# Where a tuned kernel mixes its gathered expert slots into the dense loop: a new rate, no slot step inside the last key step, and an earlier load of the first norm's weight

## The chip, the cores and the metric

The kernel runs on one core of a Trainium2 chip. The metric is the device time of one launch in microseconds. In the text PE is TensorE's matmul row, PEld its weight loads, DVE is VectorE, ACT is ScalarE, POOL is GpSimd and SP is the engine whose queue issues most loads and stores.

## The reference, cut to what matters

One layer of a decoder runs over 512 prompt tokens, 16 meta tokens and 32 sample tokens. Its last part, PEER, is what most of the change touches: each token picks 16 experts of 16384 in each of 8 heads, and adds their outputs.

```python
h = rmsnorm(x, norm1_w)                      # first norm
...
x = x + mixed @ w_out
# peer(): for each token 8 heads x 16 experts
act = gelu(einsum('thkd,td->thk', u_tab[expert], xb))
return einsum('thk,thkd->td', gate * act, v_tab[expert])
...
y = rmsnorm(x, final_norm_w)
```

## The kernel before, in words

The expert part treats tokens in two ways. Three tiles of 128 prompt tokens are **dense**: all 16384 experts are multiplied for them on PE, in 128 rows of 128 experts. A **key step** for row e (`h_step`) multiplies the row's key weights with the activations, 24 matmuls of 384 columns. A **value step** for row v (`v_step`) adds gate times gelu times value weights to the accumulators `eacc` in PSUM, 36 matmuls of 512 columns that the trace shows as 18 pairs. The two alternate from row 36 on, value row v behind key row v+1; `v_last` does the last value row, finishes the three dense tiles (`finish`: add, sum of squares on ACT, power on POOL, scale, store) and then drains what is left. All weights are fp32, split into a rounded part (`thi`, an ACT cast, L1474) and a residual (`tlo`, a DVE subtraction, L1482).

Two tiles (the 32 samples and the first prompt tile) are **gathered**: `gathered` fetches, for slot k, one expert row per token with an indirect DMA from POOL (L1338, four buffers). It then takes two steps per slot: a dot product on DVE (L1352) with gelu and gate on ACT (L1353, L1354), and one accumulation on DVE (L1359). There are 32 + 128 slots, so 320 steps, and some 15 for finishing the two tiles.

The slot steps come from the task list `fill`. Each `fill.tick(rate)` adds `rate` to a sum and emits one step for each whole unit reached. A key step has four ticks and a value step three. Every engine executes its own instructions strictly in the order in which the program emits them, so the ticks fix the place of each slot step among the dense loop's instructions on DVE and ACT.

I write one loop step of DVE as letters in program order: R is a residual (L1482), D the dot product (L1352), X the accumulation (L1359), M the gate's multiply (L1520), S the residual of the gated activation (L485). Each step begins with the R of a key row, then come the slot steps of the key step's ticks, M, R (of a value row), S, and the slot steps of the value step's ticks. Without slot steps it reads R M R S.

At the start, SP loads the sample tile, prompt tiles and the norm's weight `wbc` (L532, broadcast to 128 partitions) in the order of the calls. `norms` then runs over the tiles in a software pipeline: the sum of squares of tile i (L490 on ACT, L496 on DVE, L498 on POOL) is emitted ahead of the scaling of tile i-1 (L514 on DVE).

Of the kernel before, what the change touches and what calls it, by code (L numbers as in the profile page):

```python
# [90 lines left out]
def body(tc, a):  # L91
# [7 lines left out]
    def pool(st, name, bufs=1, right=False, space=None):  # L99
        kw = {} if space is None else {"space": space}  # L100
        return st.enter_context(tc.tile_pool(name=name, bufs=bufs, side="right" if right else "left", reuse_waits="tile", **kw))

    def load(dst, src):
        nc.sync.dma_start(dst, src)
# [399 lines left out]
    def norms(xs, xp, pm, wbc, out, hi, lo, cols, after):  # L504

        rs, hn, n = {}, {}, len(xs)
        for i in range(n + 2):
            if i < n:
                xt, k, rows = xs[i]
                rs[i] = rstd_of(xp, xt[k], rows)  # L510
            if 0 <= i - 1 < n:
                xt, k, rows = xs[i - 1]
                hn[i - 1] = out(i - 1)
                V.scalar_tensor_tensor(hn[i - 1][:rows], xt[k][:rows], rs[i - 1], wbc[:rows], ALU.mult, ALU.mult)  # L514
            if i - 2 >= 0:
                transpose_split(pm, hn[i - 2], xs[i - 2][2], hi, lo, cols[i - 2])
                after(i - 2)
# [14 lines left out]
    def load_bc(xp, name):  # L532
        t = xp.tile([P, D], F32, name="wbc", tag="wbc", bufs=1)
        load(t, a[name].to_broadcast([P, D]))
        return t
# [271 lines left out]
    def network(ph, keep_h2, wq, es, sq):  # L807
# [159 lines left out]
        with ExitStack() as xs_:  # L967
            xp = pool(xs_, "xp", 1, True)

            def fetch_x(i):  # L970
                xt = xp.tile([P, D], F32, name="xt", tag="xt", bufs=4)
                load(xt[: src[i][0]], src[i][2])
                return xt

            def after_x(i):
                if i + 4 < len(src):
                    xl.append(fetch_x(i + 4))
                if i == 0:
                    s.split(0)
                elif i == 1:  # L980
                    s.split(1)
                elif i == 2:
                    s.begin(0)
                elif i == 3:
                    s.begin(1)

            xl = [fetch_x(i) for i in range(2)]
            wbc = load_bc(xp, "n1w")
            xl += [fetch_x(i) for i in range(2, 4)]
            s.fetch(0)  # L990
            s.fetch(1)
            norms([(xl, i, r) for i, (r, _, _) in enumerate(src)], xp, pm, wbc, lambda i: xl[i], hh, hl, [c for _, c, _ in src],
                  after_x)
# [313 lines left out]
    def finish_load(o, rows, x2):  # L1307
        load(o[:rows], x2)
        return o
# [67 lines left out]
    NE = 128  # L1377
# [14 lines left out]
    Q_RATE, W_RATE = 1, 3  # L1392

    G_AHEAD = 0.38
    G_END = -8
    G_RATE = (2 * 160 + 15 - 3 * (AH - 1) * G_AHEAD) / (7 * (NE - AH) - 3 * G_END)

    def build_w(bp, pw, io, sls, Wt, w0):
# [41 lines left out]
    def experts(h2s, x2s, h2pair, ph, g_tiles, d_tiles, outs, s, ghp, es, sq):  # L1440
# [14 lines left out]
        def ps_h():  # L1455
            return php.tile([P, 512], F32, name="hps", tag="h")
# [3 lines left out]
        def fetch(kind, e):  # L1460
            if e < NE and (kind, e) not in raws:
                t = (dp if kind == "u" else dv).tile([P, D], F32, name="traw", tag="traw" + kind, bufs=2 if kind == "u" else VB)
                load(t, a["uT"][e] if kind == "u" else a["uv"][e * P : (e + 1) * P, D : 2 * D])
                raws[kind, e] = t

        def prep(kind, e, late=False):
            if e >= NE or (kind, e) in sp_:
                return
            fetch(kind, e)
            t = raws[kind, e]  # L1470
            pl, nb = (dp, 2) if kind == "u" else (wtp, VS)
            x = pl.tile([P, D], F32R, name="thi", tag="thi" + kind, bufs=nb)
            y = pl.tile([P, D], F32R, name="tlo", tag="tlo" + kind, bufs=nb)
            AC.copy(x, t)  # L1474
            sp_[kind, e] = x, y
            if not late:
                prep_lo(kind, e)

        def prep_lo(kind, e):
            if e < NE and (kind, e) in raws:  # L1480
                x, y = sp_[kind, e]
                (PO if kind == "u" and e < sum(AQ) else V).tensor_tensor(y, raws.pop((kind, e)), x, ALU.subtract)  # L1482
                if kind == "v" or e + 2 not in (AH, AH + 1) or e >= AH:
                    fetch(kind, e + (2 if kind == "u" else VB))
# [3 lines left out]
        def h_step(e, rate, lo_at=0):  # L1488
            prep("u", e)
            if e + 1 != AH:  # L1490
                fetch("u", e + 1)
                prep("u", e + 1, True)
            x, y = sp_.pop(("u", e))
            ps = ps_h()
            for k in range(KT):
                ks = slice(k * P, k * P + P)
                cs = slice(c0, c0 + nt)
                mm(ps[:, :nt], x[:, ks], hi[:, k, cs], start=(k == 0), stop=False)  # L1498
                mm(ps[:, :nt], x[:, ks], lo[:, k, cs], start=False, stop=False)  # L1499
                mm(ps[:, :nt], y[:, ks], hi[:, k, cs], start=False, stop=(k == KT - 1))  # L1500
                if k % 2:
                    (bg if e < AH else fill).tick(rate)
                if k == lo_at and e + 1 != AH:
                    prep_lo("u", e + 1)
            if e < AT:
                gh[e] = ga.tile([P, nt], F32, name="gh", tag="gh", bufs=AT)
            elif e < AH - 3:
                gh[e] = gbf[:, (e - AT) * nt : (e - AT + 1) * nt]
            else:
                gh[e] = ghp.tile([P, nt], F32, name="gh", tag="gh", bufs=3)  # L1510
            AC.activation(gh[e], ps[:, :nt], AF.Gelu)  # L1511
# [131 lines left out]
        def v_of(v, rate):  # L1643
            if v % 8 == 0:
                fetch_w(v // 8 + 1)
            v_step(v, rate)
# [15 lines left out]
        for v in range(AH - 1, NE - NL):  # L1662
            if v == AH + 1:
                load(T_["fwbc"], a["fw"].to_broadcast([P, D]))
            if v >= AH + 2 and v % 4 == 0 and late:
                i, t = late.popleft()
                fins[t] = finish_load(gb[:, i + 1], rows_of[t], x2s[t])
            if AH < v + 1 < NE:
                h_step(v + 1, G_RATE)
            v_of(v, G_RATE)  # L1670
        for v in range(NE - NL + 1, NE):
            h_step(v, G_RATE)
# [9 lines left out]
    es, sq = ExitStack(), ExitStack()  # L1682
    wq = Stream(None, None, [(WQ0 + i, None, 0, None, PO) for i in range(16)], 4, Q_RATE, 0)
    h2s, x2s, h2pair, ghp = network(ph, g_tiles, wq, es, sq)
    experts(h2s, x2s, h2pair, ph, g_tiles, d_tiles, outs, wq, ghp, es, sq)
    ctx.close()

# [91 lines left out]
```

## Time and profile before

| | us |
|---|---|
| median of 3 runs | 2202.42 (2197.52 to 2209.17) |
| the profiled execution's own time | 2195.1 |
| its span, first to last instruction | 2193.2 |
| PE busy | 2083.8 (95%) |
| PEld busy | 1916.0 (87%) |
| DVE busy | 1570.8 (72%) |
| ACT busy | 864.5 (39%) |

The dense loop with slots runs from about 1362 to 2170 us of the span, the rest of the tail to 2193.2. A busy share is an average over the whole span; which engine sets the pace of a stretch has to be read from waits.

### The profile page before, as it was taken

How to read it: one execution, taken by the hardware profiler on the slowest of the kernel's cores; microseconds unless marked ns; L12 is line 12 of the kernel's file. 1: busy time of each engine (PE TensorE's matmuls, PEld its weight loads, DVE VectorE, ACT ScalarE, POOL GpSimd, SP SyncE). 2: the span in 40 equal slices, each digit the busy share in tenths (PEclk: the TensorE clock that was granted, in tenths of full speed). 3: DMA queues.
4: the chain of work that ended last, by engine and by line, in shares of the span. 5: the costliest groups of instructions: out<-in, count | busy, mean ns of one | idle time of the engine just before them, and what ended most of it. 6: DMA issues, size and time to landing. Idle time of an engine off the chain costs nothing. (4 is left out here: it accounts for less than half of the span.)

```text
span 2193.2 us, 34559 instructions
## 1 busy us (share of the span) xinstructions
PE 2083.8 (95%) x13085; PEld 1916.0 (87%) x13085; DVE 1570.8 (72%) x3084; ACT 864.5 (39%) x1591; POOL 754.6 (34%) x875
## 2 busy tenths in 40 slices
PE   6999999999999998999899999999999999999995
PEld 6988898898999998999899878989888888888884
DVE  6866667546426314899999688778878778887877
ACT  3323343333124323333477434343433443344343
POOL 3497610025442334664166111212222222222221
PEclk9999999999999998999999999999999999999998
DMA  4433334326644233222256999879998899989884
GB/s 151 127 123 112 115 120 154 114 91 205 210 153 123 87 138 123 92 102 73 106 231 269 330 332 331 324 281 357 347 326 304 335 338 338 330 316 336 331 298 162
DMA packets 199813, 478.90 MB, mean 218 GB/s; under 512 B 53440, under 2 KB 114752, under 8 KB 176096
## 3 DMA queue, kind: packets, MB, share of 16 engines
q1 hardware_dynamic: 169136, 278.50, 37.8%
q0 software_dynamic: 24752, 170.67, 20.8%
q10 hardware_dynamic: 5760, 27.53, 3.2%
q8 instruction: 103, 1.69, 0.3%
q14 instruction: 62, 0.51, 0.1%
HBM read 419.42 MB, written 54.46 MB: 216 GB/s over the span
## 5 line engine op out<-in xcount | busy, mean ns | idle before, releaser
L471 PE MATMUL gps<-pr,wh 128*128 128x272 f32 (+1 forms) x3328 | 582.3, 297 | 6.4 <-DVE pr L485 3.8
L471 PEld LDWEIGHTS gps<-pr,wh 128*128 128x128 f32 x3328 | 479.7, 191 | 15.2 <-DVE pr L485 4.7
L1482 DVE TENSOR_TENSOR tlo<-traw,thi 128x1024 fp32r<-128x1024 f32 x241 | 299.2, 1242 | 118.1 <-ACT thi L1474 117.9
L1338 POOL DMA_INDIRECT uv<-in_uv,ei x128 | 186.2, 1455 | 534.7 <-DVE acc L1359 527.2
L1500 PE MATMUL hps<-pr,tlo 128*128 128x384 f32 x1024 | 347.7, 340 | 14.5 <-DVE tlo L1482 13.6
L471 PE MATMUL gps<-pr,wl 128*128 128x272 f32 (+1 forms) x1664 | 353.0, 293 | 2.9 <-DVE wl L437 2.2
L1498 PE MATMUL hps<-pr,thi 128*128 128x384 f32 x1024 | 350.5, 342 | 1.6 <-ACT thi L1474 1.3
L1499 PE MATMUL hps<-pr,thi 128*128 128x384 f32 x1024 | 344.1, 336 | 0.0
L1474 ACT CAST thi<-traw 128x1024 fp32r<-128x1024 f32 x256 | 266.0, 1040 | 25.5 <-PE eacc L1558 17.9
L471 PEld LDWEIGHTS gps<-pr,wl 128*128 128x128 f32 x1664 | 266.3, 192 | 3.8 <-DVE wl L437 2.9
L1558 PE MATMUL eacc<-thi,ghi 128*128 128x512 f32 x768 | 241.7, 396 | 6.8 <-ACT ghi L484 5.8
L1558 PE MATMUL eacc<-tlo,ghi 128*128 128x512 f32 x768 | 241.4, 395 | 3.4
L1558 PE MATMUL eacc<-thi,glo 128*128 128x512 f32 x768 | 237.7, 390 | 0.0
L437 POOL TENSOR_TENSOR wl<-wraw,wh 128x1024 fp32r<-128x1024 f32 x60 | 144.1, 2401 | 247.0 <-ACT wh L436 240.0
L1359 DVE SCALAR_TENSOR_TENSOR acc<-uv,w,acc 128x1024 f32<-128x1024 f32 x158 | 202.4, 1281 | 33.8 <-ACT w L1354 33.8
L1353 ACT ACTIVATE w<-w 128x1 f32<-128x1 f32 x160 | 32.5, 203 | 478.5 <-DVE uv L1352 478.5
L1500 PEld LDWEIGHTS hps<-pr,tlo 128*128 128x128 f32 x1024 | 192.6, 188 | 20.8 <-DVE tlo L1482 19.6
L1498 PEld LDWEIGHTS hps<-pr,thi 128*128 128x128 f32 x1024 | 192.7, 188 | 10.2 <-ACT thi L1474 4.5
L1499 PEld LDWEIGHTS hps<-pr,thi 128*128 128x128 f32 x1024 | 192.8, 188 | 3.5
L1352 DVE SCALAR_TENSOR_TENSOR uv<-uv,h 128x1024 f32<-128x1024 f32 x160 | 195.1, 1220 | 0.7 <-DMA uv<-in_uv,ei_None 0.7
L1558 PEld LDWEIGHTS eacc<-tlo,ghi 128*128 128x128 f32 x768 | 141.5, 188 | 46.3 <-DVE tlo L1482 17.8
L1558 PEld LDWEIGHTS eacc<-thi,ghi 128*128 128x128 f32 x768 | 140.9, 188 | 40.5 <-ACT ghi L484 16.5
(410 smaller groups left out, 3000.3 us busy)
## 6 DMA issues: line engine op xcount, KB each, us to landing
traw<-in_uT SPq DMA_DIRECT2D x128, 512.0 KB, 4.2
traw<-in_uv SPq DMA_DIRECT2D x128, 512.0 KB, 6.7
wraw<-in_W SPq DMA_DIRECT2D x104, 512.0 KB, 3.4
Wt<-wb ACTq DMA_DIRECT2D x24, 1024.0 KB, 4.4
wt<-Wt SPq DMA_DIRECT2D x15, 1536.0 KB, 14.4
st<-in_state_hgrn SPq DMA_DIRECT2D x8, 512.0 KB, 4.4
Wd<-W SPq DMA_DIRECT2D x8, 512.0 KB, 5.0
ATd<-AT SPq DMA_DIRECT2D x8, 512.0 KB, 4.2
```

The costliest lines, as they stand in the source:

```text
L437: E.tensor_tensor(wl, r3, wh, ALU.subtract)
L471: mm(ps[:, b, :w], x[:, k], y[:, k, b * w : b * w + w], start=(k == 0 and x is wh and y is hi), stop=(k == KT - 1 and x is wl))
L1338: PO.indirect_dma_start(out=uvs[j], out_offset=None, in_=a["uv"], in_offset=bass.IndirectOffsetOnAxis(ap=ei[:, k : k + 1], axis=0))
L1352: V.scalar_tensor_tensor(out=uv[:, 0:D], in0=uv[:, 0:D], scalar=1.0, in1=h2, op0=ALU.mult, op1=ALU.mult, accum_out=w)
L1353: AC.activation(w, w, AF.Gelu)
L1359: V.scalar_tensor_tensor(acc, uv[:, D:], w, acc, ALU.mult, ALU.add)
L1474: AC.copy(x, t)
L1482: (PO if kind == "u" and e < sum(AQ) else V).tensor_tensor(y, raws.pop((kind, e)), x, ALU.subtract)
L1498: mm(ps[:, :nt], x[:, ks], hi[:, k, cs], start=(k == 0), stop=False)
L1499: mm(ps[:, :nt], x[:, ks], lo[:, k, cs], start=False, stop=False)
L1500: mm(ps[:, :nt], y[:, ks], hi[:, k, cs], start=False, stop=(k == KT - 1))
L1558: mm(accs[d][:, b], l[:, ds_], r[:, b * 512 : b * 512 + 512], start=st, stop=en)
```

## The change

Three edits. The first prompt tile's load is issued behind the norm's weight rather than ahead of it. `G_END` goes from -8 to 2, which raises `G_RATE` from 295.1/668 = 0.442 to 295.1/638 = 0.463 steps per tick. And the last key step (row 127) gets rate 0 instead of `G_RATE`.

```diff
-            xl = [fetch_x(i) for i in range(2)]
+            xl = [fetch_x(0)]
             wbc = load_bc(xp, "n1w")
-            xl += [fetch_x(i) for i in range(2, 4)]
+            xl += [fetch_x(i) for i in range(1, 4)]
...
-    G_END = -8
+    G_END = 2
     G_RATE = (2 * 160 + 15 - 3 * (AH - 1) * G_AHEAD) / (7 * (NE - AH) - 3 * G_END)
...
             if AH < v + 1 < NE:
-                h_step(v + 1, G_RATE)
+                h_step(v + 1, G_RATE if v + 1 < NE - 1 else 0)
             v_of(v, G_RATE)
```

The number of instructions on DVE, PE and POOL stays the same; their order changes. The first place is DVE at the end of the loop, from the residual of key row 127 before (`traw`, `thi`, `tlo` are a weight row and its parts, `acc` is the gathered tile's sum, `gb` the tile's input and output). Before:

```order
L1482 TENSOR_TENSOR tlo<-traw,thi 128x1024
L1359 SCALAR_TENSOR_TENSOR acc<-uv,w,acc 128x1024
L1520 TENSOR_TENSOR gh<-gh,wt 128x384
L1482 TENSOR_TENSOR tlo<-traw,thi 128x1024
L485 TENSOR_TENSOR glo<-gh,ghi 128x384
L1352 SCALAR_TENSOR_TENSOR uv,w<-uv,h_9361 128x1024
L1359 SCALAR_TENSOR_TENSOR acc<-uv,w,acc 128x1024
L1352 SCALAR_TENSOR_TENSOR uv,w<-uv,h_9361 128x1024
L1359 SCALAR_TENSOR_TENSOR acc<-uv,w,acc 128x1024
L1520 TENSOR_TENSOR gh<-gh,wt 128x384
L1482 TENSOR_TENSOR tlo<-traw,thi 128x1024
L485 TENSOR_TENSOR glo<-gh,ghi 128x384
```

And now, from the last part of key row 126's step, in which the gathered tile is finished already (L1318, L496, L1324), through the rows of key row 127:

```order
L1520 TENSOR_TENSOR gh<-gh,wt 128x384
L1482 TENSOR_TENSOR tlo<-traw,thi 128x1024
L485 TENSOR_TENSOR glo<-gh,ghi 128x384
L1318 TENSOR_TENSOR gb<-gb,acc 128x1024
L496 TENSOR_SCALAR ss<-ss 128x1
L1482 TENSOR_TENSOR tlo<-traw,thi 128x1024
L1324 SCALAR_TENSOR_TENSOR gb<-gb,ss 128x1024
L1520 TENSOR_TENSOR gh<-gh,wt 128x384
L1482 TENSOR_TENSOR tlo<-traw,thi 128x1024
L485 TENSOR_TENSOR glo<-gh,ghi 128x384
L1520 TENSOR_TENSOR gh<-gh,wt 128x384
L1482 TENSOR_TENSOR tlo<-traw,thi 128x1024
```

Before, 11 slot instructions on DVE (five L1352, six L1359) stand behind the residual of key row 127, six of them behind the last S, among the finishing of the dense tiles; now none does.

The second place is DVE inside the loop, at key row 75, from one key row's residual to the next one's. Before (R D X M R S D, then R):

```order
L1482 TENSOR_TENSOR tlo<-traw,thi 128x1024
L1352 SCALAR_TENSOR_TENSOR uv,w<-uv,h_9361 128x1024
L1359 SCALAR_TENSOR_TENSOR acc<-uv,w,acc 128x1024
L1520 TENSOR_TENSOR gh<-gh,wt 128x384
L1482 TENSOR_TENSOR tlo<-traw,thi 128x1024
L485 TENSOR_TENSOR glo<-gh,ghi 128x384
L1352 SCALAR_TENSOR_TENSOR uv,w<-uv,h_9361 128x1024
L1482 TENSOR_TENSOR tlo<-traw,thi 128x1024
```

And now (R X D M R S X D, then R):

```order
L1482 TENSOR_TENSOR tlo<-traw,thi 128x1024
L1359 SCALAR_TENSOR_TENSOR acc<-uv,w,acc 128x1024
L1352 SCALAR_TENSOR_TENSOR uv,w<-uv,h_9361 128x1024
L1520 TENSOR_TENSOR gh<-gh,wt 128x384
L1482 TENSOR_TENSOR tlo<-traw,thi 128x1024
L485 TENSOR_TENSOR glo<-gh,ghi 128x384
L1359 SCALAR_TENSOR_TENSOR acc<-uv,w,acc 128x1024
L1352 SCALAR_TENSOR_TENSOR uv,w<-uv,h_9361 128x1024
L1482 TENSOR_TENSOR tlo<-traw,thi 128x1024
```

Here one slot instruction more has come between the two residuals. Over the 77 steps from the residual of key row 49 to that of key row 126, DVE's order holds six forms, this often:

| form | slot instructions | before | now |
|---|---|---|---|
| R X D M R S X | 3 | 26 | 26 |
| R D X M R S D | 3 | 25 | 22 |
| R D M R S X D | 3 | 10 | 7 |
| R X M R S D X | 3 | 9 | 3 |
| R D X M R S D X | 4 | 5 | 11 |
| R X D M R S X D | 4 | 2 | 8 |
| sum | | 238 | 250 |

The third place is SP's queue at the start, as the difference between the two:

```order
 L104 DMA xt<-in_x_sample 32x1024
-L104 DMA xt<-in_x_prompt 128x1024
 L104 DMA wbc<-in_n1w 128x1024
-L104 DMA xt<-in_x_prompt 128x1024 x2
+L104 DMA xt<-in_x_prompt 128x1024 x3
```

The weight `wbc` is now the second of the tiles' loads and the first prompt tile the third; the loads behind them keep their places.

## Rows read from the trace of the kernel before

**Rows 1.** The page: span, and busy time of each engine.
```profile
span 2193.2 us, 34559 instructions
...
PE 2083.8 (95%) x13085; PEld 1916.0 (87%) x13085; DVE 1570.8 (72%) x3084; ACT 864.5 (39%) x1591; POOL 754.6 (34%) x875
```
**Rows 2.** Busy us by stretch (PE, PEld, DVE, ACT, POOL), granted clock, DMA share, GB/s.
```profile
1480.00:2144.00 664.00, 650.00 (x3201) 569.19 (x3200) 532.34 (x656) 265.20 (x538) 169.50 (x117) 1.00 0.90 330
...
2170.00:2193.20 23.20, 0.00 (x0) 0.00 (x0) 14.52 (x21) 5.88 (x14) 3.13 (x4) 0.59 0.23 90
```
**Rows 3.** Waits of DVE, ACT, PE, 1600 to 2100 us (us, times, longest).
```profile
DVE tlo L1482 <- ACT thi L1474: 52.1, 55, 1.5
DVE gh L1520 <- ACT gh L1511: 26.3, 27, 1.0
DVE acc L1359 <- ACT w L1354: 20.3, 34, 0.6
...
ACT w L1353 <- DVE uv L1352: 273.3, 88, 3.9
...
PE hps L1500 <- DVE tlo L1482: 4.1, 7, 0.7
```
**Rows 4.** DVE in order of time, 2108 to 2154 us.
```profile
2108.25 1.22 DVE L1482 TENSOR_TENSOR tlo<-traw,thi 128x1024 fp32r<-128x1024 f32 x1 [1.53 <-ACT thi L1474]
...
2116.53 1.22 DVE L1482 TENSOR_TENSOR tlo<-traw,thi 128x1024 fp32r<-128x1024 f32 x1
...
2125.54 1.23 DVE L1482 TENSOR_TENSOR tlo<-traw,thi 128x1024 fp32r<-128x1024 f32 x1 [1.54 <-ACT thi L1474]
...
2136.59 1.23 DVE L1482 TENSOR_TENSOR tlo<-traw,thi 128x1024 fp32r<-128x1024 f32 x1 [1.53 <-ACT thi L1474]
...
2144.02 1.22 DVE L1482 TENSOR_TENSOR tlo<-traw,thi 128x1024 fp32r<-128x1024 f32 x1
...
2153.87 1.23 DVE L1482 TENSOR_TENSOR tlo<-traw,thi 128x1024 fp32r<-128x1024 f32 x1 [1.53 <-ACT thi L1474]
```
**Rows 5.** DVE in order of time: a step R D X M R S D X.
```profile
1941.55 1.22 DVE L1482 TENSOR_TENSOR tlo<-traw,thi 128x1024 fp32r<-128x1024 f32 x1
...
1950.81 1.22 DVE L1482 TENSOR_TENSOR tlo<-traw,thi 128x1024 fp32r<-128x1024 f32 x1
```
**Rows 6.** DVE in order of time: key rows 48 and 49.
```profile
1464.32 0.56 DVE L1520 TENSOR_TENSOR gh<-gh,wt 128x384 f32<-128x384 f32 x1 [2.16 <-ACT gh L1511]
...
1469.89 1.22 DVE L1482 TENSOR_TENSOR tlo<-traw,thi 128x1024 fp32r<-128x1024 f32 x1
```
**Rows 7.** The end, in order of time: PE, DVE and ACT.
```profile
2145.90 0.34 PE L1498 MATMUL hps<-pr,thi 128*128 128x384 f32 x1
...
2154.18 0.34 PE L1498 MATMUL hps<-pr,thi 128*128 128x384 f32 x1
...
2165.48 0.73 PE L1558 MATMUL eacc<-thi,ghi 128*128 128x512 f32 x2 [2.14 <-ACT ghi L484]
...
2169.61 0.39 PE L1558 MATMUL eacc<-thi,glo 128*128 128x512 f32 x1
...
2169.43 1.22 DVE L1318 TENSOR_TENSOR gb<-gb,eacc 128x1024 f32<-128x1024 f32 x1
...
2171.64 0.19 ACT L490 ACTIVATION_READ_ACCUMULATOR junk<-gb 128x1 f32 x1
...
2184.08 0.15 DVE L496 TENSOR_SCALAR ss<-ss 128x1 f32<-128x1 f32 x1
...
2184.89 1.28 DVE L1324 SCALAR_TENSOR_TENSOR gb<-gb,ss 128x1024 f32<-128x1024 f32 x1 [0.66 <-POOL ss L498]
```
**Rows 8.** The start, in order of time: ACT and DVE.
```profile
5.38 1.06 ACT L490 ACTIVATE junk<-xt 128x1024 bf16<-128x1024 f32 x1 [0.53 <-DMA xt<-in_x_prompt]
...
7.74 1.27 DVE L514 SCALAR_TENSOR_TENSOR xt<-xt,ss,wbc 32x1024 f32<-32x1024 f32 x1 [1.03 <-DMA wbc<-in_n1w]
...
10.37 0.15 DVE L496 TENSOR_SCALAR ss<-ss 128x1 f32<-128x1 f32 x1 [1.35 <-ACT junk L490]
```
## The prediction
> **What bounds the kernel now.** The page comes first: PE is busy 95% of the span and DVE 72% [rows 1], which reads like a kernel bound by matmuls. The change touches the dense loop with slots, so I read that stretch by itself: over 664 us PE is busy 650.00, its weight loads 569.19, DVE 532.34 [rows 2]. That still names PE.
>
> The waits say otherwise [rows 3]. In 500 us of the loop DVE waits only for ACT: 52.1 us for the cast `thi`, 26.3 for the gelu, 20.3 for the slot's weight, 98.7 together. And ACT's longest wait, 273.3 us, is for DVE's dot product (I found none of either engine for PE or for a transfer there). PE is the one that waits for DVE, 4.1 us for `tlo` alone. So two in-order engines hand work back and forth without regard to PE, and PE follows. The mechanism is in the code: ACT's two small instructions behind each D wait for it, and the casts and the gelu that DVE needs next stand behind those two. A D with R behind it costs a wait of 1.53 or 1.54 us [rows 4], with M behind it at most 1.0, with X behind it at most 0.6 [rows 3].
>
> The timeline confirms it. DVE takes a fixed time from one key row's residual to the next one's, whatever PE does, and it depends only on the form of the step [rows 4, 5]:
>
> - R X D M R S X: 2116.53 - 2108.25 = 8.28 us
> - R D X M R S D: 2125.54 - 2116.53 = 9.01, so 9.00 with the others
> - R X D M R S X D: 2136.59 - 2125.54 = 11.05
> - R X M R S D X: 2144.02 - 2136.59 = 7.43, taken as 7.44
> - R D M R S X D: 2153.87 - 2144.02 = 9.85
> - R D X M R S D X: 1950.81 - 1941.55 = 9.26, taken as 9.27
>
> Other steps of one form agree within 0.02 us. A check: the 77 steps from the residual at 1469.89 [rows 6] to that at 2144.02 [rows 4] last 674.13 us. The counts before give 26 x 8.28 + 25 x 9.00 + 10 x 9.85 + 9 x 7.44 + 5 x 9.27 + 2 x 11.05 = 674.19. PE alone needs 8.28 for such a step (2154.18 - 2145.90) [rows 7], so 637.6 for 77: the DVE stream is 36 us longer than PE's own work.
>
> **The change, part by part.** *The rate.* With the counts of now the same 77 steps last 26 x 8.28 + 22 x 9.00 + 7 x 9.85 + 3 x 7.44 + 11 x 9.27 + 8 x 11.05 = 694.92 us, **20.7 more**. That is for 12 slot instructions more, 1.73 us each: some 1.2 of DVE's time (an R of the same 128x1024 takes 1.22 [rows 4]) and the rest waits for ACT, since the form that multiplies most, with D as its last, is the dearest. No work of PE covers it, because PE is the one that follows.
>
> *Where the loop starts from.* The first gathered tile ends just ahead of key row 48, and there DVE has few slot steps and does wait for PE, by way of the gelu; the last such M is at 1464.32 [rows 6]. Now the tile's end comes about one step earlier, the first prompt slot with it, and that M waits for PE's row alone. From DVE's idle 2.16 us before it I take it as 0.3 us earlier; bounds 0 and 0.6. So the residual of key row 49 moves from 1469.89 to 1469.3 or so (the form around it is also 0.3 shorter), and that of key row 126 from 2144.02 to 2164.2, **+20.2 us**.
>
> *The end.* Before, 2193.2 - 2144.02 = 49.2 us follow that residual. Now PE waits for it as it does before for the residual of key row 127 at 2153.87. From there to PE's end (2169.61 + 0.39 = 2170.0) are 16.1 us, of which 2.14 are PE's wait for `ghi` of the last value row [rows 7]: its gelu stood on ACT behind two slots' weights. No slot stands there now, so the wait goes. With one step of 8.28 more, PE ends 16.1 - 2.1 + 8.3 = 22.3 us behind the residual of key row 126, less about 0.3 for matmuls that slowed at the restart: 22.0. The finished gathered tile's L1318 and L1324 on DVE, 2.5 us, lie beside 8 us of PE work here.
>
> Behind PE's end the dense tiles are finished in turn. The first can start when its accumulator is done, some 2.7 us ahead of PE's end: two of three equal parts of the last value row, which took 4.5 us with its restart (2165.48 to 2170.0). Each has a chain from its add to its scaling: the square's sum is read out 2171.64 + 0.19 - 2169.43 = 2.40 us behind the add's start, and from L496 to the scaling it takes 2184.89 - 2184.08 = 0.81, with the step between 3.3 [rows 7]. Scaling takes 1.2, and the next add stands behind it: scalings start at +0.6, +5.1 and +9.7 us of PE's end, the last of two halves ends at +11.1. Before, the last scaling ended at 2184.89 + 1.28 = 2186.17, 16.2 behind PE's end, and 7.0 us of store and end followed. I keep those 7.0. So 22.0 + 11.1 + 7.0 = 40.1 us follow the residual instead of 49.2: **-9.1 us**. Bounds: -7 if the chains meet something, -11 if the smaller last store ends sooner.
>
> *The start.* DVE waits 1.03 us for `wbc` at 7.74 [rows 8]. But the first scaling also stands behind L496 of the first prompt tile, whose load landed at 5.38 and now comes where `wbc` was. Its square (1.06) then ends near 8.9, and the first scaling starts about 1.3 us later than before instead of earlier. Little of it passes on: the second scaling stands behind L496 at 10.37, which waits for the second prompt tile, and that load keeps its place. I take +0.3 us; bounds -0.5 (the load of `wbc` was what counted) and +1.3 (all of it passes on).
>
> **Sum.** +20.2 - 9.1 + 0.3 = **+11.4 us**: span 2204.6, and the profiled execution's own 2195.1 would be 2206.5. The median shown is 2202.42, 7.3 above that execution; the difference is laid on the median: **2213.8 us**, slower by 0.52%. That is about what a measurement of this kernel can tell from no change (0.5%, 11 us).
>
> **A rule against this reading.** PE is busy 650.00 and its weight loads 569.19 of 664 us [rows 2], more than DVE. The Trainium skill (Perfetto Trace Analysis, Identifying the Most-Contended Engine) takes the engine with the highest occupancy as the one to optimize, TensorE's judged by its weight loads. By that rule PE would bind and the added DVE work would be free, which is the first rival. The waits of this trace [rows 3] disagree.
>
> **The rivals.**
> *PE hides the slots.* If DVE has slack in the loop, the 12 instructions cost nothing there and only the end counts: PE's 2.14 us wait goes and the finishing shrinks from 16.2 to 11.1, so -7.2 in all: 2195.2 us, on the other side. It decides if the mean step now stays at the 8.71 us of before (674.13 / 77). For it speak PE's 95%; against it that PE already waits for DVE. 7%.
> *Only busy time counts.* The 12 instructions cost their 1.2 us each, 14.4, and the waits for ACT stay as many as before in sum: 20.2 becomes 13.9, and the time 2207.5. For it: waits depend on neighbours, and some new pairs of forms (R D X M R S D X followed by R D X M R S D) don't occur before. Against: each form's time was the same behind every other. 14%.
> *The gathered rows come late.* A slot's buffer is fetched when the slot three ahead of it is done, and DMA is busy 0.90 of the loop [rows 2]. Three slots in a dense group now lie closer, and a D that waits 1 us for its row in each of the 12 more crowded steps adds 12 us: 2226. Against: no D waits for a transfer in the loop now, and a step is longer on the whole. 7%.
> *It doesn't do what it says.* Slots could remain behind the last key step; the order on DVE shows none. 2%: the time of before.
>
> **How the numbers follow.** My forecast has 70%, with 2209 to 2218 as its own range: bounds of the end -2 to +2, start -0.8 to +1, loop start 0.3, and 2 to 3 us for the median (the three runs shown lie 12 us apart). The range for 8 in 10 takes in the second rival and part of the third: 2205 to 2221. Slower by over 0.5% (above 2213.4): half of the forecast's 70%, a little more since 2213.8 lies above the line, and the third rival, 46%. Within 0.5%: the other half and most of the other rivals, 50%. Faster by over 0.5% (below 2191.4): 4%, from the first rival with a better end.
>
> **What would show it.** In the changed kernel's trace DVE should need 9.02 us a step (694.9 / 77), each form the time listed, and the residual of key row 126 stand near 2164. PE's busy share of the loop falls to some 95%, with all its waits for DVE and ACT. The 2.14 us wait ahead of the last value row is gone, PE ends near 2186.5, and DVE's last scaling 11 us later. The first scaling starts near 9 us. Wrong would be: steps of 8.71 (PE or slack hides), forms whose time depends on their neighbour, a D that waits for `in_uv`, or a PE start that moves by more than 1 us.

## The result, and the profile after

The changed kernel's median is 2213.0 us (2206.39 to 2221.98, 16 runs) against 2202.24 (2197.52 to 2209.17, 16 runs) of before: ratio 1.0052 [1.004, 1.0064], so 10.8 us slower. The forecast was 2213.8.

The profiled execution took 2221.98 us, 9 above its median. Its span is 26.8 us longer than the one before [rows 1], but 14.0 of these were there ahead of the loop: the residual of key row 36 stands at 1376.12, before at 1362.10. Executions differ by that much there. In the experiments e1, e2 and e8, which have the old code up to there, it stands at 1365.6 to 1368.3, and in e3, which has the new start, at 1372.79; with what each profiled execution lies off its kernel's median taken off, these four, before and after all come to 1367.0 to 1369.8. So I measure every step from a residual inside the loop. The page:

```profile
span 2220.0 us, 34561 instructions
...
PE 2100.1 (95%) x13085; PEld 1921.0 (87%) x13085; DVE 1575.1 (71%) x3084; ACT 864.4 (39%) x1591; POOL 755.6 (34%) x875
```

Busy time by stretch (PE, PEld, DVE, ACT, POOL, then granted clock, DMA share, GB/s), the loop's stretch moved by what its start moved:

```profile
1496.00:2180.00 684.00, 658.20 (x3205) 566.89 (x3203) 545.39 (x674) 268.00 (x552) 177.99 (x121) 1.00 0.89 326
```

PE is busy 96% of it, 98% before [rows 2]: the loop grew and its matmuls did not. The waits of 500 us, 1615 to 2115 (us, times, longest):

```profile
ACT w L1353 <- DVE uv L1352: 283.7, 90, 3.9
DVE tlo L1482 <- ACT thi L1474: 50.9, 55, 1.5
DVE gh L1520 <- ACT gh L1511: 28.3, 29, 1.0
DVE acc L1359 <- ACT w L1354: 20.9, 35, 0.6
...
PE eacc L1558 <- ACT ghi L484: 7.2, 14, 0.5
PE hps L1500 <- DVE tlo L1482: 7.1, 11, 0.6
```

DVE's waits for ACT are the same three with nearly the same sums (100.1 us, 98.7 in [rows 3]). What changed stands on PE: it now waits 7.1 us for `tlo` instead of 4.1, and 7.2 us for `ghi` (2.2 before). DVE's residuals of key rows 49 and 126, in order of time:

```profile
1485.79 1.23 DVE L1482 TENSOR_TENSOR tlo<-traw,thi 128x1024 fp32r<-128x1024 f32 x1 [1.54 <-ACT thi L1474]
...
2180.47 1.22 DVE L1482 TENSOR_TENSOR tlo<-traw,thi 128x1024 fp32r<-128x1024 f32 x1 [1.53 <-ACT thi L1474]
```

The 77 steps took 2180.47 - 1485.79 = 694.68 us, against 674.13 before: +20.55, and 694.92 was forecast. The forms last what they lasted before (R D X M R S D X 9.26, R X D M R S X D 11.04 and 11.05, R X D M R S X 8.28).

The start of this stretch came otherwise than forecast. DVE and ACT around key rows 47 and 48:

```profile
1462.17 0.56 DVE L1520 TENSOR_TENSOR gh<-gh,wt 128x384 f32<-128x384 f32 x1 [5.05 <-ACT gh L1511]
...
1468.08 1.23 DVE L1482 TENSOR_TENSOR tlo<-traw,thi 128x1024 fp32r<-128x1024 f32 x1 [2.16 <-ACT thi L1474]
...
1473.44 0.56 DVE L1520 TENSOR_TENSOR gh<-gh,wt 128x384 f32<-128x384 f32 x1 [0.97 <-ACT gh L1511]
...
1476.78 1.23 DVE L1482 TENSOR_TENSOR tlo<-traw,thi 128x1024 fp32r<-128x1024 f32 x1 [0.71 <-ACT thi L1474]
```
```profile
1465.96 1.06 ACT L490 ACTIVATE junk<-gb 32x1024 bf16<-32x1024 f32 x1 [2.01 <-DVE gb L1318]
...
1467.01 1.03 ACT L1474 CAST thi<-traw 128x1024 fp32r<-128x1024 f32 x1
...
1474.66 1.15 ACT L1357 ACTIVATE acc<-uv,w 128x1024 f32<-128x1024 f32 x1
1475.71 1.03 ACT L1474 CAST thi<-traw 128x1024 fp32r<-128x1024 f32 x1
```

The finished gathered tile's square (L490) and the first prompt slot's product (L1357) stand on ACT ahead of two casts, and DVE waits for both casts (2.16 and 0.71 us). In the forecast PE's row held DVE there, as in [rows 6]; here it is held one step earlier (5.05 us, at 1462.17, for a gelu that waits for PE) and the tile's end adds to the path. That is read from the trace; no run takes these two off ACT. From the residual of key row 36 to that of key row 49 it took 1485.79 - 1376.12 = 109.67 us, 1469.89 - 1362.10 = 107.79 before: +1.9 instead of -0.6. (e1, another execution of the same order, has the same 109.66.)

The end, PE and DVE in order of time:

```profile
2201.92 0.39 PE L1558 MATMUL eacc<-thi,glo 128*128 128x512 f32 x1
```
```profile
2202.88 1.28 DVE L1324 SCALAR_TENSOR_TENSOR gb<-gb,ss 128x1024 f32<-128x1024 f32 x1 [0.66 <-POOL ss L498]
...
2207.38 1.28 DVE L1324 SCALAR_TENSOR_TENSOR gb<-gb,ss 128x1024 f32<-128x1024 f32 x1 [0.66 <-POOL ss L498]
...
2211.74 1.41 DVE L1324 SCALAR_TENSOR_TENSOR gb<-gb,ss 128x512 f32<-128x512 f32 x2 [0.66 <-POOL ss L498]
```

PE shows no wait ahead of its last value row; the 2.14 us of [rows 7] are gone. It ends at 2202.31, 21.8 us behind the residual of key row 126 (forecast 22.0). The scalings start 0.6, 5.1 and 9.4 us behind that (0.6, 5.1, 9.7) and the last ends at 2213.15, +10.8 (11.1). Then 6.85 us follow (7.0). In all 39.5 us stand behind the residual of key row 126; 40.1 was forecast, 49.2 it was.

The start, ACT and DVE in order of time:

```profile
7.42 1.06 ACT L490 ACTIVATE junk<-xt 128x1024 bf16<-128x1024 f32 x1 [2.24 <-DMA xt<-in_x_prompt]
```
```profile
8.60 0.15 DVE L496 TENSOR_SCALAR ss<-ss 128x1 f32<-128x1 f32 x1 [3.24 <-ACT junk L490]
8.72 1.27 DVE L514 SCALAR_TENSOR_TENSOR xt<-xt,ss,wbc 32x1024 f32<-32x1024 f32 x1
...
10.45 1.28 DVE L514 SCALAR_TENSOR_TENSOR xt<-xt,ss,wbc 128x1024 f32<-128x1024 f32 x1 [0.28 <-POOL ss L498]
```

The wait for `wbc` of [rows 8] has become a longer one for the prompt tile's square: the first scaling starts at 8.72 instead of 7.74, behind L496 in DVE's order.

### The profile page after: what moved, and what is told of

Same layout as the page of the kernel before. It is cut to its first block, busy times and chain, and to the rows that moved or that the text cites. A ratio compares the mean times of both kernels' runs of the same rounds, so it can differ in the third digit from the quotient of the medians.

```text
span 2220.0 us, 34561 instructions
## 1 busy us (share of the span) xinstructions
PE 2100.1 (95%) x13085; PEld 1921.0 (87%) x13085; DVE 1575.1 (71%) x3084; ACT 864.4 (39%) x1591; POOL 755.6 (34%) x875
## 5 line engine op out<-in xcount | busy, mean ns | idle before, releaser
L471 PE MATMUL gps<-pr,wh 128*128 128x272 f32 (+1 forms) x3328 | 587.1, 298 | 6.4 <-DVE pr L485 3.8
L471 PEld LDWEIGHTS gps<-pr,wh 128*128 128x128 f32 x3328 | 484.2, 193 | 15.2 <-DVE pr L485 4.7
L471 PE MATMUL gps<-pr,wl 128*128 128x272 f32 (+1 forms) x1664 | 355.1, 294 | 2.8 <-DVE wl L437 2.1
L471 PEld LDWEIGHTS gps<-pr,wl 128*128 128x128 f32 x1664 | 268.6, 193 | 3.9 <-DVE wl L437 2.8
L1359 DVE SCALAR_TENSOR_TENSOR acc<-uv,w,acc 128x1024 f32<-128x1024 f32 x158 | 202.3, 1280 | 34.1 <-ACT w L1354 34.1
L1352 DVE SCALAR_TENSOR_TENSOR uv<-uv,h 128x1024 f32<-128x1024 f32 x160 | 194.8, 1217 | 0.1
L1558 PEld LDWEIGHTS eacc<-tlo,ghi 128*128 128x128 f32 x768 | 140.8, 188 | 49.5 <-DVE tlo L1482 21.8
```

Of the source, the lines that this page charges most:

```text
L471: mm(ps[:, b, :w], x[:, k], y[:, k, b * w : b * w + w], start=(k == 0 and x is wh and y is hi), stop=(k == KT - 1 and x is wl))
L1352: V.scalar_tensor_tensor(out=uv[:, 0:D], in0=uv[:, 0:D], scalar=1.0, in1=h2, op0=ALU.mult, op1=ALU.mult, accum_out=w)
L1359: V.scalar_tensor_tensor(acc, uv[:, D:], w, acc, ALU.mult, ALU.add)
L1558: mm(accs[d][:, b], l[:, ds_], r[:, b * 512 : b * 512 + 512], start=st, stop=en)
```

## The experiments

The theory is the prediction's: in the loop DVE and ACT hand work to each other in a fixed order, the order's forms set the time, and PE follows. The main rival is that PE sets it and slot work is free there.

**e1: the rate alone.**
```diff
-    G_END = -8
+    G_END = 2
```


> The rate alone (G_END 2), old start, slot rate kept in the last key step. DVE's, ACT's and PE's order is then that of the changed kernel line for line, so the last key step's zero does nothing here. My theory (in-order DVE and ACT set the loop's pace): the whole change less its start, +11 us on the kernel before (2213), the 77 steps from key row 49 to 126 in 694.8 us. Rival (the loop is PE's): -7 us.

2215.65 us (2210.93 to 2219.09, 6 runs), ratio 1.006 [1.004, 1.008]. The rate alone makes the whole change. Key row 49 to 126 takes 2172.67 - 1478.01 = 694.66 us, and 39.6 follow, as in the changed kernel. With `G_END` at 2 the task list runs out in the step of key row 126, so a rate of 0 for row 127 moves nothing: DVE, ACT, PE and POOL have the same order in the two traces.

**e2: rate 0 in the last key step alone.**
```diff
-                h_step(v + 1, G_RATE)
+                h_step(v + 1, G_RATE if v + 1 < NE - 1 else 0)
```


> Rate 0 in the last key step alone, G_END -8. One dot product and one accumulation move from ahead of the last value row's gate to the very end. My theory: loop unchanged (674.1 us for the 77 steps); PE's wait of 2.1 us for the last value row goes, but DVE's stream to the end keeps its length, since the two move behind the dense tiles' sums: -1 to +2 us. Rival (PE's end sets the end): -2 us.

2202.42 us (12 runs), ratio 0.9999 [0.9985, 1.0012]. DVE, from the first dense tile's sum on:

```profile
2169.85 1.21 DVE L1318 TENSOR_TENSOR gb<-gb,eacc 128x1024 f32<-128x1024 f32 x1
...
2184.49 1.28 DVE L1359 SCALAR_TENSOR_TENSOR acc<-uv,w,acc 128x1024 f32<-128x1024 f32 x1
...
2189.06 1.28 DVE L1324 SCALAR_TENSOR_TENSOR gb<-gb,ss 128x1024 f32<-128x1024 f32 x1 [0.66 <-POOL ss L498]
```

PE's wait of 2.14 us is gone here too: PE ends 13.6 us behind the residual of key row 127 (16.1 before). But the slot steps that stood in that key step now stand among the dense tiles' finishing, and the last scaling ends 19.5 us behind PE's end instead of 16.2. DVE's last instruction comes 33.0 us behind that residual, 32.3 before. The stall on PE was not the path.

**e3: the start alone.**
```diff
-            xl = [fetch_x(i) for i in range(2)]
+            xl = [fetch_x(0)]
             wbc = load_bc(xp, "n1w")
-            xl += [fetch_x(i) for i in range(2, 4)]
+            xl += [fetch_x(i) for i in range(1, 4)]
```


> The order of the first loads alone. My theory: the first scaling (L514) starts near 8.7 us instead of 7.7, the second one stays near 10.45, and the whole moves by -0.5 to +1 us, which is no change that can be told. Rival (the wait of 1.03 us for the weight was on the path): -1 us.

2202.26 us (12 runs), ratio 0.9998 [0.9985, 1.0012]. The first scaling starts at 8.73, the second at 10.47 (10.45 before, 10.01 to 10.23 in the other traces with the old start), and PE's first gate matmul (L471) at 17.79; kernels with the old start show 17.73 to 18.17. Of one us more on the first tile the second keeps a few tenths at most, and PE's first gate matmul none that these traces show.

**e4: three ticks for a slot.** The kernel before, with a `yield` in `gathered` between the dot product and its gelu, so that ACT's two small instructions come one tick later; the rates grow by 3/2, so that the slots end where they did.
```diff
+            yield
             AC.activation(w, w, AF.Gelu)
...
-    G_AHEAD = 0.38
+    G_AHEAD = 0.38 * 3 / 2
...
-    G_RATE = (2 * 160 + 15 - 3 * (AH - 1) * G_AHEAD) / (7 * (NE - AH) - 3 * G_END)
+    G_RATE = (3 * 160 + 15 - 3 * (AH - 1) * G_AHEAD) / (7 * (NE - AH) - 3 * G_END)
```


> The kernel before with each slot in three steps instead of two: dot product, then gelu and gate on ACT one tick later, then the accumulation; the rates are scaled by 3/2, so that a key step takes as many slots as before. Theory (ACT's two small instructions, queued behind a dot product that isn't done, hold back the casts and the gelu that DVE needs): the waits of DVE for thi and gh (78 us in 500) mostly vanish, DVE's own work of some 7 us a step falls under PE's 8.28, and the 77 steps last 638 to 645 us instead of 674: 2165 to 2172 us in all. Rival 1 (only DVE's busy time and the number of slots count, waits move elsewhere): 2195 to 2205. Rival 2 (the gathered rows' DMA, busy 0.90 of the loop, binds next): dot products wait for in_uv and the steps stay above 8.5 us.

2160.1 us (2159.05 to 2172.93, 5 runs), ratio 0.9824 [0.9798, 0.985]. Busy time of 620 us of the loop, then waits from 1600 to 2100 (the added line shifts line numbers by one):

```profile
1480.00:2100.00 620.00, 620.00 (x3147) 565.62 (x3146) 520.20 (x646) 263.57 (x528) 174.99 (x115) 1.00 0.94 347
```
```profile
...
ACT gh L1512 <- PE hps L1501: 65.1, 45, 2.5
DVE tlo L1483 <- ACT thi L1475: 43.3, 58, 1.9
DVE gh L1521 <- ACT gh L1512: 28.1, 29, 2.2
```

No work was taken away from the kernel; in the 77 steps DVE has 234 slot instructions instead of 238. PE's first matmuls of key rows 49 and 126, first before (row 126 at 2145.90, [rows 7]), then here:

```profile
1475.40 0.34 PE L1498 MATMUL hps<-pr,thi 128*128 128x384 f32 x1
```
```profile
1473.02 0.34 PE L1499 MATMUL hps<-pr,thi 128*128 128x384 f32 x1
...
2110.58 0.34 PE L1499 MATMUL hps<-pr,thi 128*128 128x384 f32 x1
```

PE's 77 steps took 670.50 us before and take 637.56 here, 33 us less. That is 8.28 a step, what PE alone needs [rows 7], and PE is busy without a gap. From key row 36 on the whole trace is 33 us shorter; the rest of the 42 us between the medians stands ahead of that row, where slots run too, and is not taken apart here. DVE's residuals of these rows are only 634.15 us apart (1468.55 to 2102.70). Where PE sets the pace, DVE can run ahead of it by more or less: PE's first matmul comes 4.47 us behind the residual of its key row at row 49 and 7.88 at row 126. So the length of such a loop has to be read on PE.

DVE's waits for `thi` and `gh` did not mostly vanish, as I had expected: 71.4 us are left of 78.4, and the time came out below my range. But ACT now waits for PE (65.1 us for `hps`), which it never did in the stretch of [rows 3]: the same rows of DVE's waits mean something else once their far end is PE. The DMA share rises to 0.94 and no D waits for its row, so the transfers had not set the pace either.

That ACT's order was the cause shows in a step that DVE runs in the same order in both, R X D M R S X. ACT in such a step, before and then here:

```profile
2111.85 0.20 ACT L1353 ACTIVATE w<-w 128x1 f32<-128x1 f32 x1 [3.63 <-DVE uv L1352]
...
2112.28 0.47 ACT L1511 ACTIVATE gh<-hps 128x384 f32<-128x384 f32 x1
```
```profile
2098.39 0.49 ACT L1512 ACTIVATE gh<-hps 128x384 f32<-128x384 f32 x1 [2.48 <-PE hps L1501]
...
2100.43 0.20 ACT L1354 ACTIVATE w<-w 128x1 f32<-128x1 f32 x1
```

Before, the gelu stands behind a small instruction that waits for D; here it stands ahead of it. DVE's waits of 0.97 us (M for the gelu) and 0.38 us (R for the cast) in that step are gone, and the step takes 6.75 us instead of 8.28, as 17 of the 25 steps of this form do here. DVE catches up in them, and in others it waits, by way of the gelu, for PE.

**e5: the change, with three ticks.** The same edit on the changed kernel.

> The changed kernel (all its three edits) with the slots in three steps. With three steps the matmuls set the loop's pace (the kernel before with three steps took 2160.1 us). Theory: the change's price came from DVE's and ACT's in-order streams setting the pace; where DVE has slack, 12 slot instructions more cost nothing in the loop and the end's gain alone is left: 5 to 8 us below 2160, so 2152 to 2155. Rival (each slot instruction in the loop costs its 1.2 to 1.7 us anyway): 2170 to 2175.

2154.32 us (2151.79 to 2159.77, 5 runs), ratio 0.9789 [0.9771, 0.9806]. The change that cost 11 us gains some 6 us here (0.9789 against 0.9824 in e4; the two intervals overlap a little). PE's first matmuls of key rows 49 and 126:

```profile
1474.81 0.34 PE L1499 MATMUL hps<-pr,thi 128*128 128x384 f32 x1
...
2113.03 0.34 PE L1499 MATMUL hps<-pr,thi 128*128 128x384 f32 x1
```

PE's 77 steps take 638.22 us, 637.56 in e4: eleven slot instructions more in DVE's stream (245 against 234) cost 0.7 us. DVE's residuals are 642.66 us apart, 8.5 more than in e4, but that is its lead over PE, which grows in e4 and shrinks here from 6.75 to 2.32 us. DVE's longest wait, 4.73 us for a cast whose weight row came late, is hidden with the rest: PE is busy 619.89 of 620 us. Behind PE's first matmul of key row 126 stand 38.5 us instead of 46.7. Together that is 7.5 us less, and the first rival's price was 7.2. So that rival was right about its condition: where PE sets the pace, nearly all of the slots' time is hidden and the shorter end counts.

**e6: less work for PE.** The kernel before without the third of the three products of the value rows (6 of the 18 matmuls of each: three dense tiles, three products, two halves of 512 columns; the text on the kernel before gives twice as many. Its output lacks that product.)
```diff
-                for l, r, st, en in ((x, vh, e == 0, False), (x, vl, False, False), (y, vh, False, e == NE - 1)):
+                for l, r, st, en in ((x, vh, e == 0, False), (x, vl, False, e == NE - 1)):
```


> The kernel before without the third of the three products of each value row (residual of the activation times rounded weights): PE's work falls by 1.37 us a step, from 8.28 to 6.9; the output lacks that product. Theory (DVE and ACT set the pace of the loop from key row 49 on): the 77 steps to the residual of key row 126 last 674 us as before, each form within 0.1 us of its time. Rival (PE sets it): they fall by up to 77 x 1.37 = 105 us, to about 570.

2196.81 us (8 runs), ratio 0.9975 [0.996, 0.999]. Busy time of 620 us of the loop, then waits from 1600 to 2100:

```profile
1480.00:2100.00 620.00, 545.35 (x2556) 448.55 (x2555) 496.47 (x613) 247.01 (x503) 159.72 (x110) 0.99 0.92 331
```
```profile
DVE tlo L1482 <- ACT thi L1474: 51.6, 54, 1.5
...
DVE gh L1520 <- ACT gh L1511: 27.3, 28, 1.0
...
PE hps L1498 <- ACT thi L1474: 23.8, 30, 1.7
PE hps L1500 <- DVE tlo L1482: 21.9, 35, 0.9
...
DVE acc L1359 <- ACT w L1354: 20.3, 34, 0.6
```

DVE's residuals of key rows 49 and 126:

```profile
1474.29 1.22 DVE L1482 TENSOR_TENSOR tlo<-traw,thi 128x1024 fp32r<-128x1024 f32 x1
...
2148.01 1.22 DVE L1482 TENSOR_TENSOR tlo<-traw,thi 128x1024 fp32r<-128x1024 f32 x1
```

This is the plainest test. PE has 12317 matmuls instead of 13085, its busy share of the loop falls from 98% to 88%, its weight loads lose a sixth, and the 77 steps take 2148.01 - 1474.29 = 673.72 us instead of 674.13. DVE's waits for ACT add up to 99.2 us, as before. All that PE was spared it spends waiting (23.8 and 21.9 us in its two longest rows). The few us that the whole kernel gained stand elsewhere, 1.9 of them between key rows 36 and 49, where DVE does wait for PE. The Trainium skill (Perfetto Trace Analysis, Identifying the Most-Contended Engine) has the engine of the highest occupancy optimized first. Here that engine lost 6 of its 42 matmuls in each step, and the loop did not change.

**e7: no power on POOL for the last tile.** e5, with the last tile's power as a square root on ACT and a reciprocal on DVE, because POOL's DRAIN at the end of the launch lasts 8.1 us and, by my theory, sets the end.
```diff
-    def rstd(sums, rows):
+    def rstd(sums, rows, last=False):
...
-        PO.tensor_tensor(r, r, mhalf[:rows], ALU.pow)
+        if last:
+            AC.activation(r, r, AF.Sqrt)
+            V.reciprocal(r, r)
+        else:
+            PO.tensor_tensor(r, r, mhalf[:rows], ALU.pow)
...
-        rr = rstd(ss, rows)
+        rr = rstd(ss, rows, n == 2)
```


> The kernel e5 with the last dense tile's power -1/2 taken as a square root on ACT and a reciprocal on DVE instead of a power on POOL. In both profiles POOL's DRAIN lasts 8.1 us from its last power on and ends 0.8 us ahead of the span's end, while SP is done 4 us earlier. Theory (that drain sets the end): the drain starts 4 us earlier, the span's end then follows the last store, and the time is 2 to 3.5 us below e5, a table load on ACT included. Rival (the end follows the last store anyway): 0 to 1.5 us above e5.

2152.36 us (2148.94 to 2156.71, 5 runs), ratio 0.9779 [0.9763, 0.9795]; with e5's interval over it the 2 us are not settled by the times. First the instructions of the launch's last line in e5, then the same in e7 (name, count, shortest/median/longest ns, first and last start):

```profile
L1776 POOLq DRAIN  x3: 46/97/8112, 2142.7 to 2151.3; - x3
L1776 SPq DRAIN  x3: 7/7/7, 2146.8 to 2151.0; - x3
```
```profile
L1780 POOLq DRAIN  x3: 46/97/8112, 2136.7 to 2146.7; - x3
L1780 SPq DRAIN  x3: 7/7/7, 2146.1 to 2146.4; - x3
```

ACT and DVE of e7 at the end:

```profile
2140.83 1.28 ACT L499 ACT_TABLE_LOAD   x1
```
```profile
2142.55 1.42 DVE L1328 SCALAR_TENSOR_TENSOR gb<-gb,ss 128x512 f32<-128x512 f32 x2
```

In the traces the mechanism holds. The record of POOL's long DRAIN starts with POOL's last power, which is now that of the tile before the last: 4.5 us behind PE's end instead of 8.8. In e5 SP's first DRAIN stands at 2146.8, about where the last store lands, and the launch ends 4.8 us after it; in e7 it stands at 2146.1, and the launch ends 0.8 us after it. So the launch ends 2.9 us behind the last scaling (2143.97 to 2146.9) instead of 6.9. The square root costs a table load of 1.28 us, which brings the last scaling 0.8 us later behind PE's end. The Trainium skill (ScalarE activation tables: per-element evaluation and per-set limits, What a function is on this engine) gives 1283 ns for such a load, and the trace agrees. e7 has the lowest median of the versions here.

**e8: a lower rate.** The kernel before with fewer slots in the loop and more behind it.
```diff
-    G_END = -8
+    G_END = -26
```


> The kernel before with G_END -26: rate 0.409, 19 slot instructions fewer in the 77 steps and as many more in the drain behind the dense tiles. By the waits seen between neighbours, the 77 steps last 647 us instead of 674.1 (8.40 a step, still over PE's 8.28); the drain grows by 9 or 10 slots of 3.03 us (1.83 from dot product to accumulation, 1.20 on to the next). Theory: +1 to +4 us on the kernel before, no change that matters. Rival (PE hides slots in the loop, so that taking them out gains nothing there): +25 us or more.

2203.64 us (12 runs), ratio 1.0013 [0.9999, 1.0028]. DVE's residuals of key rows 49 and 126:

```profile
1472.86 1.22 DVE L1482 TENSOR_TENSOR tlo<-traw,thi 128x1024 fp32r<-128x1024 f32 x1 [1.53 <-ACT thi L1474]
...
2120.75 1.23 DVE L1482 TENSOR_TENSOR tlo<-traw,thi 128x1024 fp32r<-128x1024 f32 x1 [1.54 <-ACT thi L1474]
```

The 77 steps take 647.89 us, 26.2 less than before, and 2200.7 - 2120.75 = 79.95 follow instead of 49.2, 30.7 more. The loop answers to the rate in both directions, and what leaves it comes back behind PE's end. Of the three values tried, before's -8 is at the bottom of that trade or near it: from key row 36 on, the trace with -26 is 3.6 us longer (its times can't be told from no change), and +2 costs some eleven.

## Why the prediction was right

| term | forecast | measured |
|---|---|---|
| 77 steps of the loop | +20.7 | +20.55 |
| start of these steps | -0.6 | +1.9 |
| behind the residual of key row 126 | -9.1 | -9.7 |
| start of the launch | +0.3 | not seen (e3: -0.3, interval -3 to +3) |
| sum | +11.4 | +12.8 in the traces, +10.8 in the medians |

*What bounds the loop* was the step that decided the sign. The reading from the waits, two in-order engines that hand work back and forth, is shown by e6 (less PE work, same loop) and e4 (same work, other order, a loop 33 us shorter on PE, and 1.53 us less in a step that DVE runs in the same order). "PE hides the slots" fell for this kernel, and e5 shows the condition under which it holds. The 8.28 us a step that PE alone needs, read in a loop where PE followed, is what e4 then took.

*The rate.* The time of each form and the counts of forms gave the loop within 0.3 us. "Only busy time counts" fell with it: the added slot steps cost 20.55 / 12 = 1.71 us each, not 1.2. No D waits for its gathered row in the loop, so "the gathered rows come late" fell too; in e5, whose loop is faster, a weight row came late once, and PE hid it.

*Where the loop starts from* was mis-sized. The step said that the multiply M behind the tile's end waits for PE's row alone and that an earlier end of the tile is thus free. The wait for PE came one step earlier, and the tile's square and the first product on ACT then stood on the DVE and ACT path: +1.9 us instead of -0.6. It was small, and the end came out 0.6 us better. That the median lies 0.8 us from the forecast is luck: the traces' sum is 1.4 us above the forecast's, the medians' 0.6 below it, and single executions of one kernel differ by more.

*The end* was right in each of its three parts. One attribution was loose: the wait ahead of the last value row is gone because of the rate. The edit of the last key step, of which the prediction gives no price of its own, does nothing beside it (e1), and by itself it takes the wait away without a gain (e2).

*The start* was right that the first scaling moves by about a microsecond, and that little is passed on; what is left lies under what the runs can tell.

## What to carry to other kernels

When two in-order engines feed each other, cost an interleaving by the form of the step, slot steps and waits together, and multiply by how often each form stands in the new order; busy shares said nothing here. Where PE sets the pace, measure the loop on PE, since the engines that feed it can run ahead by several us. Before filling an engine's gaps, ask which engine its waits end at: the same rows of DVE's waits for ACT came from ACT's queue order in one kernel and from PE in the next, and the same change cost 11 us in the one and gained 6 in the other. And before moving work among the loop, look whether a small instruction that waits holds up a large one behind it: one `yield`, with the rates scaled to it, was worth some four times what the rate cost (42 us against 11).

## What was unexpected of the hardware

A DRAIN on POOL at the end of the launch lasts 8.11 to 8.13 us in each of these traces, and its record starts with POOL's last power (0.04 us ahead of it). So the time of that last power sets the launch's end even where the stores are done earlier: with it in the last tile 6.9 us pass from the last scaling to the end (e5), with it moved off POOL there 2.9 (e7).
